# Seven block products for fourteen of sixteen pairs in the second product of an MLP

## The chip, the cores and the metric

The kernel runs on one core of one Trainium2 chip. The metric is the device time of one execution in microseconds (us), as the median over repeated executions. A core has TensorE (matrix products, writing to PSUM), VectorE, ScalarE and GpSimd for elementwise work, and SyncE, which issues the transfers between device memory and SBUF in this kernel. In the rows of the profile they are called PE (PEld for the loading of weights), DVE, ACT, POOL and SP. Each engine works through its own instructions in order and waits on the others by semaphores.

## The reference

One layer of a diffusion backbone: a recurrent branch and a Fourier branch, merged and projected, and then an MLP. The part that matters here is the MLP on 1024 tokens of width 1024, hidden width 4096:

```
h   = modulate(rms_norm(x), shift, scale)
act = square(relu(h @ w1))          # 1024 x 4096
x   = x + gt2 * (act @ w2)          # gt2: one gate per output column
out = rms_norm(x, g_final)
```

All data is float32.

## The kernel before

*How a product is formed.* A float32 operand is split into two parts of TensorE's `fp32r` format: `hi`, a copy rounded by ScalarE, and `lo`, the remainder, subtracted by VectorE (`split`, L97 to L98). A product is three passes (hi x hi, hi x lo, lo x hi), each a matmul of 128 x 128 weights against 128 x 512 columns, added up in PSUM.

*First product of the MLP* (class `Pair`, L906 to L1005). It runs over 16 pairs of feature tiles (a feature tile is 128 hidden features), each pair by seven block products instead of eight (the products `p1` to `p7`, 12 matmuls each). Each pair's results come together on VectorE: L986, L987, L993 and L1000 add PSUM banks into f1 and f2, L1004 squares the positive part, and L1005 stores a feature tile of `act` to device memory (`act_d`). `out3` finishes f1 and `out4` f2. The loop over pairs is a hand-written order: inside `tc.manual_schedule` the instructions of TensorE, VectorE and ScalarE stand as they are written, while SyncE and GpSimd are placed by a scheduler.

*Second product* (L1076 to L1144). Everything here is placed by the scheduler. It goes over 8 chunks of CH = 4 feature tiles. For each feature tile `load_split` (L757) loads the tile of `act_d` and the rows of `w2` into a working tile (`wr`), multiplies the `w2` rows by the gate `gt2` (L761, VectorE) and splits both (L98). For each of the eight output tiles (128 tokens x 1024 columns) the chunk's matmuls (L1099, 24 per output tile) add up in a PSUM tile (`mm`), and VectorE adds that to `x2` (L1136), which already holds the residual. So `x2` is the accumulator, read and written in each chunk. In the last chunk each output tile is finished at once by `finish`: square sum (L217, ScalarE), root and reciprocal (L211, L212), scaling (L1108) and store (L1109). The last output tile is taken in two halves (L1144 to L1152), so that its store starts early.

*Space.* SBUF pages come from pools: `pg` (by `page`), `yp` (by `ypage`, 17 of 4 KB per partition) and `wp`. PSUM holds 8 banks: in the first product as 8 single banks (`bk`), in the second as 4 tiles of two banks (`mm`, the pool "psum2"). A new tile waits until the old contents of its place have been read.

Of the kernel before, what the change touches and what calls it, by code (L numbers as in the profile page):

```python
# [17 lines left out]
F32 = mybir.dt.float32  # L18
# [6 lines left out]
P = 128  # L25
# [25 lines left out]
def block_kernel(es: ExitStack, tc: tile.TileContext, a, out):  # L51
# [27 lines left out]
    def page(shape, dt=F32, pool=None, tag="s"):  # L79
        return (pool or pg).tile(shape, dt, tag=tag, name=nm("pg"))  # L80
# [70 lines left out]
    def passes(w, x):  # L151
        return ((w[0], x[0]), (w[0], x[1]), (w[1], x[0]))
# [594 lines left out]
    with tc.tile_pool(name="yp", bufs=17, reuse_waits="tile") as yp:  # L747
        def ypage(shape, dt=F32):
            return page(shape, dt, yp, "y")
# [156 lines left out]
        class Pair:  # L906
# [96 lines left out]
            def put_out(self, t, j):  # L1003
                V.scalar_tensor_tensor(t, t, 0.0, t, ALU.max, ALU.mult)  # L1004
                dma(act_d[2 * self.n + j], t)  # L1005

        NP = FF // P // 2
        pr = [Pair(n) for n in range(NP)]
        with tc.high_priority(offset=PRIO):
# [68 lines left out]


        for i in range(KT):  # L1080
            x2[i] = page([P, D])
            dma(x2[i], x2_d[i])

        def load_act(f):
            hi, lo = ypage([P, T], F32R), ypage([P, T], F32R)
            load_split(act_d[f], hi, lo)
            return hi, lo

        def load_w2(f):
            hi, lo = page([P, D], F32R), page([P, D], F32R)  # L1090
            load_split(a["w2"][f * P:(f + 1) * P], hi, lo, gt2)
            return hi, lo

        def ff2(ps, i, f0, f1, hs=(0, 1)):
            for f in range(f0, f1):
                l2 = [t[:, i * P:(i + 1) * P] for t in av[f]]
                for j, (l, r) in enumerate(passes(l2, wv[f])):
                    for h in hs:
                        PE.matmul(ps[h], l, r[:, h * HB:(h + 1) * HB],  # L1099
                                  start=f == 0 and j == 0, stop=f == CH - 1 and j == 2)  # L1100

        def halves(ps):
            return ps[:, 0:HB], ps[:, HB:2 * HB]

        def finish(i):
            square_sum(x2[i], ssf[:, i:i + 1])
            r = rstd(ssf[:, i:i + 1])
            V.scalar_tensor_tensor(x2[i], x2[i], r, gfin, ALU.mult, ALU.mult)  # L1108
            dma(out[i * P:(i + 1) * P], x2[i])  # L1109

        CH = 4
        NC = FF // P // CH
        ssf = tiny(8)
        for c in range(NC):
            av, wv = [], []
            for f in range(CH):
                with tc.high_priority(offset=PRIO):
                    av.append(load_act(c * CH + f))
                    wv.append(load_w2(c * CH + f))
            pss = [mm_ps() for _ in range(2)]  # L1120
            for f0, f1 in ((0, CH - 1), (CH - 1, CH)):
                for i in range(2):
                    ff2(halves(pss[i]), i, f0, f1)
            if c == NC - 1:
                gfin = wr_tile()
                dma(gfin, a["g_final"].partition_broadcast(P))
            for i in range(KT):
                if c == NC - 1 and i == KT - 1:
                    psl = [mm_ps()[:, 0:HB] for _ in range(2)]
                    for h in range(2):  # L1130
                        ff2(psl, i, 0, CH, (h,))
                else:
                    if i >= 2:
                        pss.append(mm_ps())
                        ff2(halves(pss[i]), i, 0, CH)
                    V.tensor_tensor(x2[i], x2[i], pss[i], ALU.add)  # L1136
                if c == NC - 1 and i:
                    finish(i - 1)
        i = KT - 1
        hs = (slice(0, HB), slice(HB, D))  # L1140
        xg = wr_tile()
# [101 lines left out]
```

## Time and profile of the kernel before

| | |
|---|---|
| median of 3 runs | 1492.56 us (1491.32 to 1495.24) |
| the profiled execution | 1492.06 us |
| its span, first to last instruction | 1490.3 us |
| mean granted clock of TensorE | 0.989 |
| PE busy | 1433.6 us (96%) |
| PEld busy | 1163.7 us (78%) |
| DVE busy | 975.3 us (65%) |
| ACT busy | 552.7 us (37%) |
| POOL busy | 13.0 us (1%) |

Busy times are sums over the whole span; the second product of the MLP fills the last 365 us of it. An engine's busy share says little by itself: what matters in a stage is which engine the others wait for. [...]

### The profile page before, as it was taken

How to read it: one execution, taken by the hardware profiler on the slowest of the kernel's cores; microseconds unless marked ns; L12 is line 12 of the kernel's file. 1: busy time of each engine (PE TensorE's matmuls, PEld its weight loads, DVE VectorE, ACT ScalarE, POOL GpSimd, SP SyncE). 2: the span in 40 equal slices, each digit the busy share in tenths (PEclk: the TensorE clock that was granted, in tenths of full speed). 3: DMA queues.
4: the chain of work that ended last, by engine and by line, in shares of the span. 5: the costliest groups of instructions: out<-in, count | busy, mean ns of one | idle time of the engine just before them, and what ended most of it. 6: DMA issues, size and time to landing. Idle time of an engine off the chain costs nothing. (4 is left out here: it accounts for less than half of the span.)

```text
span 1490.3 us, 16239 instructions
## 1 busy us (share of the span) xinstructions
PE 1433.6 (96%) x6520; PEld 1163.7 (78%) x6520; DVE 975.3 (65%) x1141; ACT 552.7 (37%) x683; POOL 13.0 (1%) x14
## 2 busy tenths in 40 slices
PE   4999999999999999999995999999998999999998
PEld 3888888888888877888774778888877888888886
DVE  7664648888987898546566776666677654455524
ACT  7443245775576647221244212222223221112102
POOL 0000000000000000000002000000000000000000
PEclk9999999999999999999997999999999999999999
DMA  8433611334224334649321343322358332133202
GB/s 326 182 113 117 236 43 57 115 129 144 82 90 129 116 123 131 206 129 338 113 96 36 132 141 105 102 106 97 105 171 294 128 103 75 51 111 113 71 0 113
DMA packets 54475, 188.89 MB, mean 127 GB/s; under 512 B 6084, under 2 KB 6492, under 8 KB 54400
## 3 DMA queue, kind: packets, MB, share of 16 engines
q1 hardware_dynamic: 54399, 187.86, 36.9%
q8 instruction: 51, 0.84, 0.2%
q14 instruction: 25, 0.20, 0.0%
HBM read 150.60 MB, written 37.23 MB: 126 GB/s over the span
## 5 line engine op out<-in xcount | busy, mean ns | idle before, releaser
L1099 PE MATMUL mm<-pg,pg 128*128 128x512 f32 x1536 | 358.5, 396 | 3.9 <-DVE pg L98 3.9
L1099 PEld LDWEIGHTS mm<-pg,pg 128*128 128x128 f32 x1536 | 289.6, 189 | 72.6 <-DVE pg L98 4.3
L321 PE MATMUL mm<-pg,wh 128*128 128x512 f32 x1120 | 309.1, 397 | 0.5 <-DVE pg L98 0.5
L321 PEld LDWEIGHTS mm<-pg,wh 128*128 128x128 f32 x1120 | 204.9, 189 | 44.0 <-DVE pg L98 1.4
L958 PE MATMUL bk<-pg,wh 128*128 128x512 f32 x720 | 226.0, 395 | 2.2 <-DVE wr L297 1.1
L98 ACT ACTIVATE pg<-wr 128x1024 fp32r<-128x1024 f32 (+1 forms) x114 | 102.8, 932 | 272.0 <-PE mm L1099 166.9
L321 PE MATMUL mm<-pg,wl 128*128 128x512 f32 x560 | 175.4, 394 | 0.0
L1136 DVE TENSOR_TENSOR pg<-pg,mm 128x1024 f32<-128x1024 f32 x63 | 76.2, 1218 | 132.2 <-PE mm L1099 132.1
L958 PEld LDWEIGHTS bk<-pg,wh 128*128 128x128 f32 x720 | 134.9, 188 | 35.2 <-DVE wr L297 2.1
L958 PE MATMUL bk<-pg,wl 128*128 128x512 f32 x360 | 141.6, 393 | 0.0
L98 DVE TENSOR_TENSOR pg<-wr,pg 128x1024 fp32r<-128x1024 f32 (+1 forms) x114 | 121.2, 1087 | 29.8 <-ACT pg L98 29.4
L98 DVE TENSOR_TENSOR wl<-wr,wh 128x1024 fp32r<-128x1024 f32 (+2 forms) x73 | 81.6, 1120 | 75.8 <-ACT wh L98 75.8
L98 ACT ACTIVATE wh<-wr 128x1024 fp32r<-128x1024 f32 (+2 forms) x73 | 71.0, 975 | 147.8 <-PE mm L321 68.5
L321 PEld LDWEIGHTS mm<-pg,wl 128*128 128x128 f32 x560 | 105.4, 188 | 24.2
L859 PE MATMUL mm<-pg,pg 128*128 128x512 f32 x384 | 91.9, 397 | 0.0
L958 PE MATMUL bk<-pg,pg 128*128 128x512 f32 x264 | 73.3, 429 | 19.2 <-ACT pg L98 15.1
L859 PEld LDWEIGHTS mm<-pg,pg 128*128 128x128 f32 x384 | 71.0, 188 | 17.8 <-DVE g L893 2.2
L958 PEld LDWEIGHTS bk<-pg,pg 128*128 128x128 f32 x264 | 53.2, 206 | 36.0 <-ACT pg L98 19.0
L958 PEld LDWEIGHTS bk<-pg,wl 128*128 128x128 f32 x360 | 67.6, 188 | 16.0
L98 ACT ACTIVATE wh<-pg 128x1024 fp32r<-128x1024 f32 x32 | 33.6, 1063 | 112.1 <-PE bk L958 52.7
L776 PE MATMUL mm<-pg,wh 128*128 128x512 f32 x256 | 70.0, 394 | 1.7 <-ACT pg L98 1.7
L217 ACT ACTIVATE jk<-pg 128x1024 bf16<-128x1024 f32 (+1 forms) x27 | 27.6, 1021 | 108.3 <-DVE pg L1136 66.9
(231 smaller groups left out, 1679.9 us busy)
## 6 DMA issues: line engine op xcount, KB each, us to landing
wr<-in_w SPq DMA_DIRECT2D x67, 512.0 KB, 4.1
wr<-in_win SPq DMA_DIRECT2D x36, 512.0 KB, 4.4
pg<-in_wm SPq DMA_DIRECT2D x32, 512.0 KB, 8.3
wr<-in_wm SPq DMA_DIRECT2D x32, 512.0 KB, 3.8
act_d<-pg SPq DMA_DIRECT2D x32, 512.0 KB, 2.8
wr<-act_d SPq DMA_DIRECT2D x32, 512.0 KB, 4.2
pg<-in_x SPq DMA_DIRECT2D x16, 512.0 KB, 8.0
gyb_d<-l SPq DMA_DIRECT2D x8, 512.0 KB, 4.0
```

What stands on the lines that cost most here:

```text
L98: return S.activation(hi, src, AF.Copy), V.tensor_tensor(lo, src, f32(hi), ALU.subtract)
L217: S.activation(j[:, 0:src.shape[1]], src, AF.Square, accum_out=dst)
L321: PE.matmul(ps[:, h * HB:(h + 1) * HB], l[:, k, :], r[:, h * HB:(h + 1) * HB], start=k == 0 and i == 0, stop=k == KT - 1 and i == 2)
L776: PE.matmul(ps[:, h * HB:(h + 1) * HB], l[:, k, :], r[:, h * HB:(h + 1) * HB], start=k == 0 and i == 0, stop=k == KT - 1 and i == 2)
L859: PE.matmul(ps, l, r, start=k == 0 and j == 0, stop=k == KT - 1 and j == 2)
L958: PE.matmul(ps, l, r, start=first and k == 0 and i == 0, stop=k == 3 and i == 2, skip_group_check=not first)
L1099: PE.matmul(ps[h], l, r[:, h * HB:(h + 1) * HB], start=f == 0 and j == 0, stop=f == CH - 1 and j == 2)
L1136: V.tensor_tensor(x2[i], x2[i], pss[i], ALU.add)
```

## The change

The second product is written anew as a class `Mlp2`. Take a pair of feature tiles. Its `act` part is a 2 x 2 matrix of blocks (two halves of the tokens, two feature tiles), its `w2` part another (two feature tiles, two halves of the columns). The product of the two is formed by seven block products (Strassen's scheme in Winograd's form), for 14 of the 16 pairs. The pairs are taken in three chunks of 5, 5 and 4; the seven products of a chunk are *units* (`units`, 21 of them), and a unit is 12 matmuls per pair, added up over the pairs of the chunk in two PSUM tiles.

- *Operands.* Four loads per pair bring page tiles x, y, z, w of 1024 columns, each holding a 512-column block of `act_d` and a 512-column block of `w2` (L1042, L1043: DMAs of 256 KB with rows of 2 KB). Sums and differences of blocks are formed in place: L1068, L1070, L1072 on VectorE (1024 wide), L1074 and L1076 on GpSimd (512 wide). Each unit's operands are split (L98) into a ring of 17 tiles.
- *Accumulators.* Each of the seven products has two tiles `acc` of 1024 columns in SBUF. After a unit ScalarE copies PSUM there in the first chunk (L1094), and VectorE adds PSUM to it in the two others (L1096).
- *End.* 14 additions (L1107) turn the seven accumulators into four blocks; GpSimd multiplies them by the gate (L1113, 16 times 512 wide). The last two pairs, four feature tiles, are taken plainly as before (`plain`, `plain_mm`, gated on GpSimd, L1119). Per output tile VectorE adds two halves of accumulators (L1163) and a PSUM tile (L1167) to `x2`, and `finish` (L1014, L1015) follows.
- *Order.* `begin()` (loads, first splits and sums) is written ahead of `pr[15].out4()`, and all of `run()` lies inside the manual schedule. The gain `g_final` is loaded into `gacc`.

```diff
+        class Mlp2:
+            CHUNKS, NPL = ((0, 5), (5, 5), (10, 4)), 2
+            SRC = {"x": (0, 0, 1, 1), "y": (1, 0, 0, 1), "z": (1, 1, 0, 0), "w": (0, 1, 1, 0)}
+            RING = ("wr",) * 4 + ("y",) * 3 + ("wh", "wl") * 3 + ("s",) * 4
...
+            def load(self, c, names, new=page, ks=None):
+                n0, g = self.CHUNKS[c]
+                for k in ks or range(g):
+                    for n in names:
+                        r, ca, cb, d = self.SRC[n]
+                        t = self.src[c][n][k] = new([P, 2 * HB])
+                        f = 2 * (n0 + k)
+                        dma(t[:, 0:HB], act_d[f + ca][:, r * HB:(r + 1) * HB])
+                        dma(t[:, HB:], a["w2"][(f + cb) * P:(f + cb + 1) * P, d * HB:(d + 1) * HB])
...
+                    if u == 1:
+                        p["s"][k] = page([P, 2 * HB])
+                        V.tensor_tensor(p["s"][k], x, y, ALU.subtract)
+                    elif u == 2:
+                        V.tensor_tensor(y, y, z, ALU.add)
+                    elif u == 3:
+                        V.tensor_tensor(y, y, x, ALU.subtract)
+                    elif u == 4:
+                        G.tensor_tensor(z[:, HB:], w[:, HB:], y[:, HB:], ALU.subtract)
+                    elif u == 5:
+                        G.tensor_tensor(x[:, 0:HB], w[:, 0:HB], y[:, 0:HB], ALU.subtract)
...
+            def evac(self, i):
...
+                for j, ps in enumerate(self.ps.pop(i)):
+                    if c == 0:
+                        self.acc[u].append(ypage([P, 2 * HB]))
+                        S.activation(self.acc[u][j], ps, AF.Copy)
+                    else:
+                        V.tensor_tensor(self.acc[u][j], self.acc[u][j], ps, ALU.add)
+
+            def begin(self):
+                self.load(0, "xz", ypage, range(2))
+                self.load(0, "xz", page, range(2, 5))
+                self.split(0)
+                self.load(0, "y")
+                self.sums(1)
...
+            def gate(self, u, d):
+                for j in range(2):
+                    t = self.acc[u][j].rearrange("p (a b) -> p a b", b=HB)
+                    for h in range(2):
+                        G.tensor_tensor(t[:, h], t[:, h], gt2[:, d * HB:(d + 1) * HB], ALU.mult)
+
+            def plain(self, f):
...
+                G.tensor_tensor(rw, rw, gt2, ALU.mult)
...
+            def run(self):
...
+                for i, (c, u) in enumerate(self.units):
+                    self.evac(i - 1)
+                    if u == 1:
+                        self.load(c, "w")
+                    if u >= 4 and c + 1 < nc_:
+                        self.load(c + 1, "xyz"[u - 4])
+                    self.split(i + 1)
+                    self.sums(i + 2)
+                    if c + 1 == nc_ and u >= 3:
+                        self.plain(f0 + u - 3)
+                    self.mm(i)
...
+                self.comb(Q6, Q6, Q1, ALU.add)
+                self.comb(Q7, Q6, Q7, ALU.subtract)
+                self.comb(Q4, Q4, Q7, ALU.add)
+                self.gate(Q4, 0)
+                self.comb(Q7, Q5, Q7, ALU.subtract)
+                self.gate(Q7, 1)
+                self.comb(Q2, Q2, Q1, ALU.add)
+                self.gate(Q2, 0)
+                self.comb(Q5, Q5, Q6, ALU.subtract)
+                self.evac(nu - 1)
+                self.comb(Q3, Q3, Q5, ALU.add)
+                self.gate(Q3, 1)
+                C = ((Q2, Q3), (Q4, Q7))
+                for n, i in enumerate(order):
+                    for h in range(2):
+                        s = slice(h * HB, (h + 1) * HB)
+                        t = self.acc[C[i // 4][h]][i % 4 // 2][:, i % 2 * HB:(i % 2 + 1) * HB]
+                        V.tensor_tensor(x2[i][:, s], x2[i][:, s], t, ALU.add)
+                    if n < KT - 1:
+                        ps = mm_ps()
+                        self.plain_mm(halves(ps), i, (0, 1))
+                        V.tensor_tensor(x2[i], x2[i], ps, ALU.add)
...
+                    if n:
+                        finish(order[n - 1])
...
+            mlp2.begin()
             pr[NP - 1].out4()
-        psum_pool("psum2", 4)
...
+            psum_pool("psum2", 4)
+            mlp2.run()
```

What the change moves is seen in the order of three engines. First SyncE's transfers around the store of the last pair's first feature tile (`act_d<-pg_7932` before, `act_d<-pg_7933` now, both L1005). Before, loads of the residual (`x_d`) and of the next feature tiles stand there:

```order
L759 DMA wr_8086<-act_d 128x1024
L1082 DMA pg_8028<-x_d 128x1024
L1082 DMA pg_8030<-x_d 128x1024
L759 DMA wr_8092<-in_w 128x1024
L1005 DMA act_d<-pg_7932 128x1024
L1082 DMA pg_8032<-x_d 128x1024
L1005 DMA act_d<-pg_7965 128x1024
```

Now (pg_8081 is the y tile of the first pair, pg_8042 and pg_8048 are z tiles, pg_8045 an x tile):

```order
L1042 DMA pg_8039<-act_d 128x512
L1043 DMA pg_8039<-in_w 128x512
L1005 DMA act_d<-pg_7933 128x1024
L1042 DMA pg_8042<-act_d 128x512
L1043 DMA pg_8042<-in_w 128x512
L1042 DMA pg_8045<-act_d 128x512
L1043 DMA pg_8045<-in_w 128x512
L1042 DMA pg_8048<-act_d 128x512
L1043 DMA pg_8048<-in_w 128x512
L1042 DMA pg_8081<-act_d 128x512
L1043 DMA pg_8081<-in_w 128x512
```

The first loads of the stage stand on both sides of the store; three of the ten x and z tiles and all y tiles stand behind it.

Then VectorE at the end of the first product. Before, with bk_7938 and bk_7952 the PSUM banks of the last pair:

```order
L987 TENSOR_TENSOR pg_7965<-pg_7965,bk_7952 128x512
L98 TENSOR_TENSOR pg_8085<-wr_8086,pg_8084 128x1024
L1000 TENSOR_TENSOR pg_7932<-pg_7933,bk_7952 128x512
L1004 SCALAR_TENSOR_TENSOR pg_7932<-pg_7932 128x1024
L993 TENSOR_TENSOR pg_7965<-pg_7933,bk_7938 128x512
L1004 SCALAR_TENSOR_TENSOR pg_7965<-pg_7965 128x1024
L761 TENSOR_TENSOR wr_8092<-wr_8092,gt_5873 128x1024
L98 TENSOR_TENSOR pg_8052<-wr_8053,pg_8051 128x1024
```

Now, with bk_7939 the bank that L993 reads and pg_8081 to pg_8093 the y tiles:

```order
L1004 SCALAR_TENSOR_TENSOR pg_7933<-pg_7933 128x1024
L98 TENSOR_TENSOR wr_8052<-pg_8021,wr_8051 128x512
...
L98 TENSOR_TENSOR wh_8076<-pg_8048,wl_8075 128x512
L1068 TENSOR_TENSOR pg_8096<-pg_8021,pg_8081 128x1024
L1068 TENSOR_TENSOR pg_8098<-pg_8027,pg_8084 128x1024
L1068 TENSOR_TENSOR pg_8100<-pg_8033,pg_8087 128x1024
L1068 TENSOR_TENSOR pg_8102<-pg_8039,pg_8090 128x1024
L1068 TENSOR_TENSOR pg_8104<-pg_8045,pg_8093 128x1024
L993 TENSOR_TENSOR pg_7966<-pg_7934,bk_7939 128x512
L1004 SCALAR_TENSOR_TENSOR pg_7966<-pg_7966 128x1024
```

L993 and the second L1004 stood right behind the first L1004; now ten half splits and five sums stand between them.

Last, VectorE at the end of the second product. Before, an addition of PSUM, a reciprocal and a scaling for each output tile:

```order
L1136 TENSOR_TENSOR pg_8032<-pg_8032,mm_9978 128x1024
L212 RECIPROCAL tiny_10039<-tiny_10039 128x1
L1108 SCALAR_TENSOR_TENSOR pg_8032<-pg_8032,tiny_10039,wr_9967 128x1024
L1136 TENSOR_TENSOR pg_8034<-pg_8034,mm_10011 128x1024
L212 RECIPROCAL tiny_10072<-tiny_10072 128x1
```

Now, behind ten further L1107 (mm_9974 and mm_9975 belong to the last block product, mm_10075 and mm_10103 to plain products, x_1503 and x_1504 are output tiles):

```order
L1107 TENSOR_TENSOR pg_8397<-pg_8397,pg_8488 128x1024
L1107 TENSOR_TENSOR pg_8399<-pg_8399,pg_8490 128x1024
L1096 TENSOR_TENSOR pg_8811<-pg_8811,mm_9974 128x1024
L1096 TENSOR_TENSOR pg_8813<-pg_8813,mm_9975 128x1024
L1107 TENSOR_TENSOR pg_8811<-pg_8811,pg_8397 128x1024
L1107 TENSOR_TENSOR pg_8813<-pg_8813,pg_8399 128x1024
L1163 TENSOR_TENSOR x_1503_10032<-x_1503_10032,pg_8589 128x512
L1163 TENSOR_TENSOR x_1503_10032<-x_1503_10032,pg_8306 128x512
L1167 TENSOR_TENSOR x_1503_10032<-x_1503_10032,mm_10075 128x1024
L1163 TENSOR_TENSOR x_1504_10034<-x_1504_10034,pg_8589 128x512
```

The additions of the last block product's PSUM tiles stand behind twelve L1107, and each output tile has two more additions.

## Rows read from the trace of the kernel before

**Rows 1.** The costliest groups of the page: busy us, mean ns | idle before, releaser.
```profile
L1099 PE MATMUL mm<-pg,pg 128*128 128x512 f32 x1536 | 358.5, 396 | 3.9 <-DVE pg L98 3.9
```
**Rows 2.** The chain that ended last, its last 400 us: start us, us, what.
```profile
1108.67 1.13 DVE wr L761
1109.81 0.61 DVE pg L977
...
1110.55 11.35 PE bk L958 x48
...
1121.92 0.70 DVE pg L993
...
1122.65 1.23 DVE pg L1004
1123.87 1.14 DVE wr L761
1125.01 1.15 DVE pg L98
...
1126.20 357.91 PE mm L1099 x1534
...
1484.13 0.70 DVE pg L1144
```
**Rows 3.** Busy time of each engine by stretches.
```profile
core 0: us, PE busy (x) PEld busy (x) DVE busy (x) ACT busy (x) POOL busy (x), PEclk, DMA share, GB/s
650.00:655.00 5.00, 5.00 (x23) 4.03 (x23) 2.43 (x3) 2.05 (x3) 0.00 (x0) 1.00 0.81 223
790.00:795.00 5.00, 4.59 (x10) 3.20 (x11) 1.57 (x2) 0.61 (x2) 0.00 (x0) 0.50 0.38 108
795.00:800.00 5.00, 4.80 (x23) 3.57 (x22) 2.51 (x3) 2.59 (x5) 1.29 (x1) 0.93 0.00 0
1126.20:1131.80 5.60, 5.60 (x17) 4.44 (x18) 3.35 (x3) 0.00 (x0) 0.00 (x0) 0.70 0.97 364
1131.00:1136.00 5.00, 5.00 (x24) 4.02 (x23) 0.00 (x0) 0.00 (x0) 0.00 (x0) 1.00 1.03 419
1200.00:1300.00 100.00, 100.00 (x432) 80.89 (x432) 49.49 (x42) 16.09 (x16) 0.00 (x0) 1.00 0.27 85
```
**Rows 4.** Timeline of DVE at the end of the first product: start us, us.
```profile
1119.16 0.69 DVE L1000 TENSOR_TENSOR pg<-pg,bk 128x512 f32<-128x512 f32 x1
1119.88 1.23 DVE L1004 SCALAR_TENSOR_TENSOR pg<-pg 128x1024 f32<-128x1024 f32 x1
```
**Rows 5.** Transfers of the page: count, KB each, us from issue to landing.
```profile
act_d<-pg SPq DMA_DIRECT2D x32, 512.0 KB, 2.8
```
**Rows 6.** Groups by line and form from 1050 us to the end.
```profile
L98 DVE TENSOR_TENSOR pg<-wr,pg 128x1024 fp32r<-128x1024 f32 x64 | 76.2, 1221 | 26.5 <-ACT pg L98 26.3
L1136 DVE TENSOR_TENSOR pg<-pg,mm 128x1024 f32<-128x1024 f32 x63 | 76.2, 1218 | 132.2 <-PE mm L1099 132.1
L98 ACT ACTIVATE pg<-wr 128x1024 fp32r<-128x1024 f32 x64 | 64.5, 1053 | 229.5 <-PE mm L1099 166.9 <-DMA wr<-act_d 56.6 <-DVE wr L761 5.8
L761 DVE TENSOR_TENSOR wr<-wr,gt 128x1024 f32<-128x1024 f32 x32 | 39.1, 1222 | 9.6 <-DMA wr<-in_w 9.5
L1108 DVE SCALAR_TENSOR_TENSOR pg<-pg,tiny,wr 128x1024 f32<-128x1024 f32 x7 | 9.0, 1284 | 0.2
```
**Rows 7.** Timeline of PE after two pauses, their idle time in brackets.
```profile
790.18 1.22 PE L958 MATMUL bk<-pg,pg 128*128 128x512 f32 x2 [7.18 <-ACT pg L98]
...
1121.73 0.62 PE L1099 MATMUL mm<-pg,pg 128*128 128x512 f32 x2
1126.20 9.03 PE L1099 MATMUL mm<-pg,pg 128*128 128x512 f32 x31 [3.85 <-DVE pg L98]
```
**Rows 8.** Timeline of POOL, 820 to 835 us.
```profile
825.40 1.29 POOL L842 TENSOR_TENSOR wr<-pg 128x512 f32<-128x512 f32 x1 [10.12 <-issue]
827.32 1.67 POOL L845 TENSOR_TENSOR wr<-pg,wr 128x512 f32<-128x512 f32 x1 [0.63 <-DVE wr L844]
```
**Rows 9.** Timeline of DVE beside it, 820 to 830 us.
```profile
824.63 0.69 DVE L843 TENSOR_TENSOR wr<-pg,pg 128x512 f32<-128x512 f32 x1 [5.86 <-ACT pg L823]
825.43 1.81 DVE L844 TENSOR_TENSOR wr<-pg,wr 128x512 f32<-128x512 f32 x1
...
828.37 1.71 DVE L98 TENSOR_TENSOR pg<-wr,pg 128x1024 fp32r<-128x1024 f32 x1 [0.52 <-ACT pg L98]
```
**Rows 10.** The queue of SP at the end.
```profile
1486.84 0.81 SPq L1152 DMA_DIRECT2D out<-wr  x2
```

More of the change, by code (lines that the diff above doesn't have):

```diff
@@ L1005, in put_out, with halves, finish, __init__ @@
                 dma(act_d[2 * self.n + j], t)
+        def halves(ps):
+            return ps[:, 0:HB], ps[:, HB:2 * HB]
+        def finish(i):
+            square_sum(x2[i], ssf[:, i:i + 1])
+            r = rstd(ssf[:, i:i + 1])
+            V.scalar_tensor_tensor(x2[i], x2[i], r, gfin, ALU.mult, ALU.mult)
+            dma(out[i * P:(i + 1) * P], x2[i])
+        class Mlp2:
+            CHUNKS, NPL = ((0, 5), (5, 5), (10, 4)), 2
+            SRC = {"x": (0, 0, 1, 1), "y": (1, 0, 0, 1), "z": (1, 1, 0, 0), "w": (0, 1, 1, 0)}
+            RING = ("wr",) * 4 + ("y",) * 3 + ("wh", "wl") * 3 + ("s",) * 4
+            def __init__(self):
+                self.units = [(c, u) for c in range(len(self.CHUNKS)) for u in range(7)]
+                self.src = [{n: [None] * g for n in "xyzws"} for _, g in self.CHUNKS]
+                self.op, self.ps, self.acc, self.slot = {}, {}, [[] for _ in range(7)], 0
+            def ring(self):
+                tag = self.RING[self.slot % len(self.RING)]
+                self.slot += 1
+                if tag in ("y", "s"):
+                    return (ypage if tag == "y" else page)([P, 2 * HB], F32R)
+                return wp.tile([P, 2 * HB], F32R, tag=tag, name=nm(tag), bufs=4 if tag == "wr" else 3)
+            def load(self, c, names, new=page, ks=None):
[7 more added lines that the diff above has]
+                        dma(t[:, HB:], a["w2"][(f + cb) * P:(f + cb + 1) * P, d * HB:(d + 1) * HB])
+            def split(self, i):
+                if i >= len(self.units):
+                    return
+                c, u = self.units[i]
+                p, self.op[i] = self.src[c], []
+                for k in range(self.CHUNKS[c][1]):
+                    hi, lo = self.ring(), self.ring()
+                    if u == 0:
+                        split(p["x"][k][:, 0:HB], hi[:, 0:HB], lo[:, 0:HB])
+                        split(p["z"][k][:, HB:], hi[:, HB:], lo[:, HB:])
+                    else:
+                        split(p["_syyzwx"[u]][k], hi, lo)
+                    self.op[i].append((hi, lo))
+            def sums(self, i):
+                if i >= len(self.units):
+                    return
+                c, u = self.units[i]
+                p = self.src[c]
+                for k in range(self.CHUNKS[c][1]):
+                    x, y, z, w = (p[n][k] for n in "xyzw")
+                    if u == 1:
[9 more added lines that the diff above has]
+                        G.tensor_tensor(x[:, 0:HB], w[:, 0:HB], y[:, 0:HB], ALU.subtract)
+            def mm(self, i):
+                self.ps[i] = [mm_ps() for _ in range(2)]
+                op, t = self.op.pop(i), [h for ps in self.ps[i] for h in halves(ps)]
+                for k, hl in enumerate(op):
+                    for j in range(4):
+                        m = [q[:, j * P:(j + 1) * P] for q in hl]
+                        for n, (l, r) in enumerate(passes(m, [q[:, HB:] for q in hl])):
+                            PE.matmul(t[j], l, r, start=k == 0 and n == 0, stop=k == len(op) - 1 and n == 2)
+            def evac(self, i):
+                if i < 0:
+                    return
+                c, u = self.units[i]
+                for j, ps in enumerate(self.ps.pop(i)):
+                    if c == 0:
+                        self.acc[u].append(ypage([P, 2 * HB]))
+                        S.activation(self.acc[u][j], ps, AF.Copy)
+                    else:
+                        V.tensor_tensor(self.acc[u][j], self.acc[u][j], ps, ALU.add)
[5 more added lines that the diff above has]
+                self.sums(1)
+            def comb(self, d, s0, s1, op):
+                for j in range(2):
+                    V.tensor_tensor(self.acc[d][j], self.acc[s0][j], self.acc[s1][j], op)
+            def gate(self, u, d):
+                for j in range(2):
+                    t = self.acc[u][j].rearrange("p (a b) -> p a b", b=HB)
+                    for h in range(2):
+                        G.tensor_tensor(t[:, h], t[:, h], gt2[:, d * HB:(d + 1) * HB], ALU.mult)
+            def plain(self, f):
+                ra, rw = page([P, T]), page([P, D])
+                dma(ra, act_d[f])
+                dma(rw, a["w2"][f * P:(f + 1) * P])
+                G.tensor_tensor(rw, rw, gt2, ALU.mult)
+                t = [page([P, T], F32R) for _ in range(4)]
+                split(ra, t[0], t[1])
+                split(rw, t[2], t[3])
+                self.pl.append((t[:2], t[2:]))
+            def run(self):
+                nu, nc_, self.pl = len(self.units), len(self.CHUNKS), []
+                f0 = 2 * sum(self.CHUNKS[-1])
+                for i, (c, u) in enumerate(self.units):
[9 more added lines that the diff above has]
+                    self.mm(i)
+                order = (4, 5, 6, 7, 0, 1, 2, 3)
+                Q1, Q7, Q5, Q6, Q4, Q2, Q3 = range(7)
+                for j in range(KT):
+                    x2[j] = wp.tile([P, D], F32, tag=self.RING[(0, 1, 2, 3, 7, 8, 9, 10)[j]], name=nm("x2"),
+                                    bufs=4 if j < 4 else 3)
+                    dma(x2[j], x2_d[j])
+                dma(gfin, a["g_final"].partition_broadcast(P))
+                self.comb(Q6, Q6, Q1, ALU.add)
[20 more added lines that the diff above has]
+                        V.tensor_tensor(x2[i], x2[i], ps, ALU.add)
+                    else:
+                        self.last = i, [mm_ps()[:, 0:HB] for _ in range(2)]
+                        for h in range(2):
+                            self.plain_mm(self.last[1], i, (h,))
+                    if n:
+                        finish(order[n - 1])
+            def plain_mm(self, ps, i, hs):
+                for f, (av, wv) in enumerate(self.pl):
+                    for j, (l, r) in enumerate(passes([t[:, i * P:(i + 1) * P] for t in av], wv)):
+                        for h in hs:
+                            PE.matmul(ps[h], l, r[:, h * HB:(h + 1) * HB],
+                                      start=f == 0 and j == 0, stop=f == 2 * self.NPL - 1 and j == 2)
@@ L1007, in block_kernel @@
+        ssf, gfin, mlp2 = tiny(8), gacc, Mlp2()
         NP = FF // P // 2
@@ L1094, in ff2 @@
[L1094 to L1138, printed above, removed]
@@ L1139, in block_kernel @@
-        i = KT - 1
+            psum_pool("psum2", 4)
+            mlp2.run()
+        i, psl = mlp2.last
         hs = (slice(0, HB), slice(HB, D))
-        xg = wr_tile()
+        xg = ypage([P, D])
         st = tiny(2)
```

11 lines of the change are left out of this document (removed).

## The prediction

> **What bounds the kernel now.** I read the costliest groups of the page first: the 1536 matmuls of the second MLP product (L1099) hold TensorE for 358.5 us, with 3.9 us of idle time ahead of them [rows 1]. The chain of waits comes next. The reader is to see that from 1126.20 us one block of 357.91 us, all L1099, runs to the end, that ahead of it stand four VectorE operations (1121.92 to 1126.15) during which TensorE waits, and behind it a short tail [rows 2]. The stage table comes third: in the steady stretch 432 matmuls pass in 100 us, 0.2315 us each, with VectorE 49% and ScalarE 16% busy and GpSimd idle [rows 3]. So the stage is bound by TensorE. VectorE has about 50 us of slack in each 100, and a change that trades matmuls for VectorE work is paid out of that slack until it is used up.
>
> **The change, part by part.** I call E the end of the last matmul of the first product: 1121.90 in the chain. One wait ahead of it, 1109.81 to 1110.55 on L977, stands behind a gate and a split of the old stage (L761, L98) [rows 2]. In the new order of VectorE these two no longer stand ahead of L977, so I take E = 1121.2.
>
> *Matmuls.* 14 pairs x 7 products x 12 are 1176, and four plain feature tiles x 8 x 2 x 3 are 192: 1368 instead of 1536. 168 x 0.232 = 39.0 us saved. A matmul is the same 128x512 instruction as before.
>
> *Start of the stage.* SP's order decides it. The store of the last pair's first feature tile (waiting for L1004, which ends 0.8 us before E [rows 4]) stands ahead of six loads of x and z and of the ten loads of y; with the store these are 4.6 MB. VectorE's order does the rest: the five sums of L1068, which need y, stand ahead of the last pair's L993. TensorE's 7th matmul of the new stage writes a PSUM tile over the bank that L993 reads. So TensorE does 6 matmuls behind E and then waits for the fifth y, one sum and L993. In the first 10 us of the old stage the queues moved 364 to 419 GB/s at a DMA share near 1 [rows 3]: 11 to 13 us, and with 2 to 2.8 us of flight (a 512 KB store lands 2.8 behind its issue [rows 5]) the last y is there at E + 12.5 to 15. A sum takes 1.22 (as L1136 does [rows 6]) and L993 0.69 [rows 2]: I take a restart at E + 15.5. The price on the other side: these loads have rows of half the length, and in a stretch that mixes such loads with long ones 223 GB/s went with a share of 0.81, 275 at a full share [rows 3]; that gives E + 20. I take the value near the first rows, since the burst is the same kind as theirs. Idle time is then 15.5 - 1.4 = 14.1 against 3.85 before, the gap between 1126.20 and the first two matmuls of L1099 [rows 7].
>
> After 7.2 us of idle time [rows 7] the granted clock was 0.50 over 790 to 795 and 0.93 over the next 5 us, some 2.8 us lost; before, in the first 5.6 us of L1099, 0.70, so 1.7 lost [rows 3]. The start costs 10.2 + 1.1 = 11.3 us more than now.
>
> *The block products.* A unit is one of the seven products of a chunk: with five pairs 60 matmuls, 13.95 us. VectorE does in a unit at most 10 splits or sums of 1024 elements at 1.22 and two additions of PSUM at 1.22 [rows 6]: 14.6. GpSimd gets 10 subtractions of 512 per chunk at 1.29 each [rows 8], 4 plain gates, and later 16 gates. In the trace these two engines don't run beside each other: while GpSimd's L842 ran (825.40 to 826.69) VectorE's L844 took 1.81, and a 512-wide operation otherwise takes 0.69 [rows 8, 9]; a split beside L845 took 1.71 instead of 1.22. Where operations follow each other, they start 1.14 apart [rows 2]. So a GpSimd operation between SBUF tiles is counted on VectorE's time. The additions of PSUM read one SBUF operand less; I count them as free of this.
>
> [...]
>
> Added up unit by unit, the first two chunks (c0's sums go to ScalarE) leave VectorE behind by no unit's length, so no matmul waits. In the third chunk, with four pairs and 11.16 us a unit, six units give 67 us of matmuls; VectorE has 12 additions, 24 splits, 8 sums and 8 plain splits, 62.7 us, and GpSimd 8 x 1.29 + 4 x 2.5 = 20.3, of which 4.5 lie beside additions of PSUM: 78.5. VectorE starts the last unit 11.5 us late. Stalls inside the stage: 0 to 2 us, I take 1.
>
> *The tail.* Before, TensorE set the pace to the last matmul, and 6.2 us followed. Now VectorE does. From the start of the last block product (call it T): 11.5 of arrears; 12 of 14 additions L1107 between SBUF tiles, 12 x 1.14 = 13.7; beside them seven gates of GpSimd at 1.29, 9.0; two additions of PSUM, 2.4; the last two L1107 and two gates, 4.9; then eight result tiles, each with two 512-wide additions, one of PSUM and one L1014 (1.28, as L1108 [rows 6]). The first two tiles 6.6 and four of the gates left 5.2, 11.8; five more at 0.69 x 2 + 1.22 + 1.28 and a reciprocal, about 4 each, 19.9; the last with its halves and its own scaling 6.9, the store 3.25 (from 1486.84 to the span's end at 1490.3, about the same [rows 10]). Sum: 83.3, say 84. TensorE alone would need 48 + 192 matmuls, 55.7, and 6.2 behind them: 62. TensorE is held in the middle of it: four PSUM tiles exist, so its third plain tile waits for the additions of PSUM that stand behind twelve L1107. The tail costs 22 us more than TensorE's own pace.
>
> *Edits at about nothing.* The earlier load of the final gain and the loads of x2 have over 60 us of lead. ScalarE has 42 more splits and 14 copies, at 1.05 each [rows 6] some 60 us over 270, beside matmuls: its busy share stays below 50%, and if it were late a unit's split would move by one operation, 1 us. The 32 gates of w2 (39.1 us, L761) leave VectorE; they lay beside matmuls and give nothing by themselves.
>
> *Sum.* E 1121.2, restart 1136.7; then 1176 - 6 - 48 = 1122 matmuls at 0.232, 260.3, plus 2.8 of clock and 1 of stalls: T = 1400.8. T + 84 = 1484.8 for the span, against 1490.3: 5.5 less. The same from the terms: -39.0 - 0.7 + 11.3 + 1 + 22 = -5.4. The profiled execution took 1492.06, 1.8 outside its span and 0.5 below the median of 1492.56. So I forecast **1487 us** (1492.06 - 5.5 = 1486.6).
>
> **The rivals.**
> *GpSimd beside VectorE costs little.* If the two met only at the start of an operation, the 20.3 us of the third chunk's GpSimd work and the gates of the tail would fall out of VectorE's path: arrears of 11.5 gone, 9.0 less in the gates, and TensorE's 62 as the floor: about 17 us less, 1470. Against it stand both meetings of rows 8 and 9, which agree to 0.1 us. Chance 0.15.
> *The start is no longer than now.* If y came in time, 10.6 us fall away: 1476.5. That needs loads issued before E, and SP's order has them behind the store. Chance 0.07.
> *Slower: GpSimd also holds the additions of PSUM, and an operation costs it more than 1.29.* L845 took 1.67 where it met VectorE [rows 8]. With 1.65 each, 24 operations of 512 from the third chunk on cost 8.6 more, the plain gates 2.9, and the 4.5 of overlap and the additions between the gates, some 6 in all, go: 17 to 18 more, 1504. It decides from about 1.45 per operation with the overlap gone (24 x 0.16 + 4 x 0.32 = 5.1, and a part of the 6): the gain of 5.5 is then used up. For it speaks that all of VectorE's slack is planned away; against it that 1.67 contains the wait for a split. Chance 0.20.
> *That it doesn't do what it says:* the order holds 1368 matmuls, so this has no chance worth a number.
> The forecast keeps 0.58, between 1480 and 1494 by its own bounds: the start E + 13.5 to E + 20 (-2, +4.5), arrears and stalls 4 either way.
>
> **How the numbers follow.** 0.3%, about 4.5 us, is what a measurement of this kernel can tell from no change, so *faster* is below 1488 and *slower* above 1497. Faster: 0.15 + 0.07 and 0.32 of the forecast's 0.58, 0.54. Same: 0.22 of the forecast and 0.03 of the slower rival, 0.25. Slower: 0.04 and 0.17, 0.21. The range 1471 to 1503 leaves out half of the first rival and half of the slower one.
>
> **What would show it right or wrong.** In the profile after: 1368 matmuls in two groups; one gap of 13 to 15 us on TensorE ahead of the 7th matmul, released by L993, with L1068 waiting for loads of y; clock near 0.5 for about 5 us; matmuls without gaps over 260 us; GpSimd's 512-wide operations at 1.29 to 1.7 and VectorE's neighbours of them at about 1.8; VectorE idle less than a few us from the third chunk to the end; idle time on TensorE at the third plain tile, released by L1096 or L1167. Wrong if the gap at the start is below 6 or over 20 us, if matmuls wait inside chunks, or if VectorE finishes the last block product's additions before T + 30.

## The result and the profile after

The changed kernel takes **1470.57 us** (median of 4 runs, 1469.69 to 1471.51), the kernel before 1492.05 beside it: a ratio of 0.9852 (95% interval 0.9835 to 0.9869). The forecast was 1487, with a range from 1471 to 1503. The sign was right, and the gain four times the forecast's 5.5 us: the profiled execution took 1469.69 with a span of 1467.9, 22.4 less than 1490.3.

First the start of the stage, in the chain that ended last (start us, us, what). It answers to [rows 2]:

```profile
1094.99 24.76 PE bk L958 x107
...
1122.20 6.27 DMA pg<-in_w
...
1128.49 5.42 DMA pg<-in_w
...
1134.03 1.23 DVE pg L1068
...
1135.31 1.23 DVE pg L1068
...
1136.54 0.61 DVE pg L993
```

and in TensorE's timeline, which answers to [rows 7]:

```profile
1119.57 0.40 PE L1085 MATMUL mm<-wr 128*128 128x512 f32 x1
1120.29 0.72 PE L1085 MATMUL mm<-wr,wr 128*128 128x512 f32 x2 [0.32 <-DVE wr L98]
...
1137.19 0.79 PE L1085 MATMUL mm<-wr 128*128 128x512 f32 x1 [15.48 <-DVE pg L993]
```

The reader is to see the loads of y, the last two sums, L993, and TensorE waiting 15.48 us for it behind 6 matmuls: the forecast's gap, with its restart at 1137.19 against 1136.7.

Then the stages (columns as in [rows 3]):

```profile
1137.20:1142.80 5.60, 5.60 (x15) 4.39 (x16) 5.60 (x5) 1.06 (x1) 0.00 (x0) 0.56 0.61 167
1200.00:1300.00 100.00, 100.00 (x437) 81.78 (x436) 74.24 (x65) 45.07 (x49) 22.69 (x10) 1.00 0.32 107
1331.10:1397.10 66.00, 66.00 (x290) 53.97 (x289) 65.84 (x49) 27.43 (x27) 27.89 (x12) 1.00 0.25 89
1402.10:1415.80 13.70, 13.70 (x61) 11.11 (x60) 13.70 (x14) 0.00 (x0) 7.84 (x1) 1.00 0.36 136
1415.80:1442.50 26.70, 26.70 (x117) 21.66 (x116) 25.12 (x19) 4.34 (x9) 26.68 (x16) 1.00 0.06 25
```

TensorE has no gap in any of them; 437 matmuls pass in 100 us where 432 did [rows 3]. In the third chunk (third line) VectorE is busy all the time, 49 operations in 66 us. Behind the restart the granted clock, a share of full speed, was 0.56 over 5.6 us (first line): 5.6 x 0.44, 2.5 us lost.

The tail shows what was not foreseen. VectorE's timeline:

```profile
1402.12 13.71 DVE L1107 TENSOR_TENSOR pg<-pg,pg 128x1024 f32<-128x1024 f32 x12
1415.75 2.35 DVE L1096 TENSOR_TENSOR pg<-pg,mm 128x1024 f32<-128x1024 f32 x2
1418.02 3.56 DVE L1107 TENSOR_TENSOR pg<-pg,pg 128x1024 f32<-128x1024 f32 x2
1421.49 1.79 DVE L1163 TENSOR_TENSOR x<-x,pg 128x512 f32<-128x512 f32 x1
1424.48 1.77 DVE L1163 TENSOR_TENSOR x<-x,pg 128x512 f32<-128x512 f32 x1 [1.20 <-POOL pg L1113]
```

GpSimd's timeline beside it, the first gate, and below it the start of its first run in the first chunk:

```profile
1407.96 9.03 POOL L1113 TENSOR_TENSOR pg<-pg,gt 128x512 f32<-128x512 f32 x1 [8.11 <-DVE pg L1107]
```

```profile
1161.29 5.47 POOL L1074 TENSOR_TENSOR pg<-pg,pg 128x512 f32<-128x512 f32 x1 [333.89 <-DVE pg L1072]
1166.72 1.30 POOL L1076 TENSOR_TENSOR pg<-pg,pg 128x512 f32<-128x512 f32 x1
1167.97 2.35 POOL L1074 TENSOR_TENSOR pg<-pg,pg 128x512 f32<-128x512 f32 x1
1170.28 2.28 POOL L1076 TENSOR_TENSOR pg<-pg,pg 128x512 f32<-128x512 f32 x1
```

Twelve L1107 took 13.71 us, 1.14 each, although a gate had been waiting since 1407.96. That gate lasted 9.03 us: it ended with the first addition of PSUM, behind the twelve. Only then do the engines take turns: L1163 at 1.79 instead of 0.68, which it takes behind the last gate. The same is to be seen in the first chunk: 5.47 for the first L1074, until the last of five L1072 in a row was done, and 2.3 each once VectorE works again.

TensorE was never held in the tail: the 192 plain matmuls run from 1408.11 without a wait for 44.7 us, to 1452.8. VectorE goes on for 11.5 us behind that, and the end comes with it.

### The profile page after: what moved, and what is told of

Same layout as the page of the kernel before. It is cut to its first block, busy times and chain, and to the rows that moved or that the text cites. A ratio compares the mean times of both kernels' runs of the same rounds, so it can differ in the third digit from the quotient of the medians.

```text
span 1467.9 us, 16270 instructions
## 1 busy us (share of the span) xinstructions
PE 1390.6 (95%) x6352; PEld 1131.4 (77%) x6352; DVE 1058.0 (72%) x1209; ACT 611.2 (42%) x753; POOL 123.6 (8%) x62
## 5 line engine op out<-in xcount | busy, mean ns | idle before, releaser
L98 DVE TENSOR_TENSOR wl<-wr,wh 128x1024 fp32r<-128x1024 f32 (+2 forms) x73 | 81.6, 1121 | 75.5 <-ACT wh L98 75.5
L98 ACT ACTIVATE wh<-wr 128x1024 fp32r<-128x1024 f32 (+2 forms) x73 | 71.0, 976 | 147.6 <-PE mm L321 67.0
L98 ACT ACTIVATE pg<-pg 128x1024 fp32r<-128x1024 f32 (+4 forms) x86 | 75.7, 901 | 64.5 <-PE mm L1085 13.3
L98 ACT ACTIVATE wh<-pg 128x1024 fp32r<-128x1024 f32 x48 | 50.2, 1061 | 125.7 <-PE bk L958 52.6
L98 DVE TENSOR_TENSOR pg<-pg,pg 128x1024 fp32r<-128x1024 f32 (+4 forms) x71 | 81.0, 1157 | 20.0 <-ACT pg L98 19.9
L859 PE MATMUL mm<-pg,pg 128*128 128x512 f32 x384 | 91.9, 397 | 0.0
L859 PEld LDWEIGHTS mm<-pg,pg 128*128 128x128 f32 x384 | 71.0, 188 | 17.9 <-DVE g L893 2.2
L98 DVE TENSOR_TENSOR wl<-pg,wh 128x1024 fp32r<-128x1024 f32 x48 | 58.0, 1223 | 28.0 <-ACT wh L98 28.0
L1074 POOL TENSOR_TENSOR pg<-pg,pg 128x512 f32<-128x512 f32 x14 | 37.5, 2676 | 476.8 <-DVE pg L1072 476.8
L842 POOL TENSOR_TENSOR wr<-pg 128x512 f32<-128x512 f32 x4 | 5.7, 1424 | 810.5 <-ACT pg L823 800.5
L1085 PE MATMUL mm<-pg,pg 128*128 128x512 f32 x224 | 69.7, 392 | 0.0
```

The source lines that it names most:

```text
L98: return S.activation(hi, src, AF.Copy), V.tensor_tensor(lo, src, f32(hi), ALU.subtract)
L842: G.tensor_tensor(t34[:, 0], b22, b12, ALU.subtract)
L859: PE.matmul(ps, l, r, start=k == 0 and j == 0, stop=k == KT - 1 and j == 2)
L1074: G.tensor_tensor(z[:, HB:], w[:, HB:], y[:, HB:], ALU.subtract)
L1085: PE.matmul(t[j], l, r, start=k == 0 and n == 0, stop=k == len(op) - 1 and n == 2)
```

## The experiments

The times below are medians beside runs of the kernel before (1493.34 for e1 to e3, 1492.93 for e5 and e6, 1492.10 for e7), so ratios are to be compared, with 0.9852 for the changed kernel; gains in us are taken from them. The three small kernels (m1 to m3) were executed once each. The question was whether the forecast's rule (each GpSimd operation costs VectorE its 1.29 us) or another one rules the two engines, and how much of the time the start and the gates hold.

**Turns, measured by themselves (m1_turns).**

```
for i in range(12):
    V.tensor_tensor(A[i], A[i], B, ALU.add)      # or another kind
    if i == 1: gates()                           # 6 GpSimd products of 128x512
```

> A kernel of its own, without the layer: blocks of 12 VectorE operations of 128x1024, beside 6 GpSimd products of 128x512 that start behind the second of them. Adds between SBUF tiles alone; GpSimd alone; the same adds beside GpSimd; subtractions with a rounded result, without a wait on another engine; adds that wait for ScalarE copies made long before; adds of a PSUM tile; adds with a one-element operation between them. The forecast's rule (each GpSimd operation costs VectorE 1.29 us): the 12 take 13.7 + 6 x 1.29 = 21.4 us in every block but the ones alone and with PSUM. Theory of turns (a run of VectorE operations that waits for no other engine keeps GpSimd out; one that waits for another engine lets it in): the plain run takes 13.7 us and the first contending GpSimd operation lasts over 8 us, the rounded run the same, and the run that waits for ScalarE alternates: about 2.3 us for each VectorE and each GpSimd operation while both go on, some 20 us in all. If it is the rounded result that lets GpSimd in, the rounded run alternates and the waiting one doesn't. PSUM: 13.7 us and GpSimd at 1.29 each, or, if additions of PSUM contend too, as one of the others.

VectorE's blocks (start us, us):

```profile
19.18 13.68 DVE L56 TENSOR_TENSOR acc<-acc,bop 128x1024 f32<-128x1024 f32 x12
...
40.55 20.10 DVE L64 TENSOR_TENSOR acc<-acc,bop 128x1024 f32<-128x1024 f32 x12
...
60.71 20.09 DVE L71 TENSOR_TENSOR rem<-acc,bop 128x1024 fp32r<-128x1024 f32 x12
...
80.80 13.70 DVE L77 TENSOR_TENSOR acc<-acc,cop 128x1024 f32<-128x1024 f32 x12
...
101.82 13.65 DVE L83 TENSOR_TENSOR acc<-acc,mm 128x1024 f32<-128x1024 f32 x12
```

GpSimd's beside the plain adds, the waiting adds and the adds of PSUM:

```profile
43.05 2.11 POOL L47 TENSOR_TENSOR gat<-acc,gt 128x512 f32<-128x512 f32 x1 [2.61 <-DVE acc L64]
45.12 11.04 POOL L49 TENSOR_TENSOR gat<-gat,gt 128x512 f32<-128x512 f32 x5
...
83.28 12.33 POOL L47 TENSOR_TENSOR gat<-acc,gt 128x512 f32<-128x512 f32 x1 [9.24 <-DVE acc L77]
...
104.31 1.27 POOL L47 TENSOR_TENSOR gat<-acc,gt 128x512 f32<-128x512 f32 x1 [2.60 <-DVE acc L83]
```

Three things follow. In turns six gates cost VectorE 20.10 - 13.68 = 6.4 us, 1.07 each, not 1.29. Twelve additions of PSUM lose nothing beside six gates, 13.65 against 13.68 for the plain adds alone, and GpSimd beside them nothing either: 1.27 for the first gate, 1.26 alone. And a run can keep GpSimd out (12.33 for the first gate, VectorE at 13.70) - but in the block where my theory of turns expected turns, and not in the plain one where it expected none. That theory fell.

In the block with 12.33 GpSimd waited not for one operation of VectorE but for ten, to the end of the run at 94.50.

**The start (e1_out4_second).**

```diff
-            mlp2.begin()
-            pr[NP - 1].out4()
+            mlp2.begin(pr[NP - 1].out4)
...
                     self.op[i].append((hi, lo))
+                    if between and k == 0:
+                        between()
```

> The changed kernel with out4 of the last pair written behind the first pair's half splits, ahead of the other splits and the five sums. Theory (the start waits for L993 behind the loads of y, 15.5 us idle and 2.5 of clock): the gap falls to 0 to 3 us, the block products start at once, y is there before the second unit needs it, and the time falls by 13 to 17 us, to about 1455. Rival (y is late for the second unit too, the wait only moves): a gap of over 8 us before the second unit and a gain under 7 us.

Measured 1459.07, ratio 0.9769 (0.9755 to 0.9784), 12 us faster than the changed kernel. The gap of 15.48 is gone; TensorE's timeline has in its place, ahead of the second unit:

```profile
1139.84 0.50 PE L1087 MATMUL mm<-wh,wl 128*128 128x512 f32 x1 [3.90 <-DVE wh L98]
```

That split stands behind five sums, the last of which waits for the last load of y. The stage behind it (columns as in [rows 3]):

```profile
1139.80:1145.40 5.60, 5.56 (x17) 4.43 (x18) 5.60 (x6) 1.82 (x2) 0.00 (x0) 0.70 0.63 229
```

The gain is less than the 13 to 17 us expected, and the rows say why: the wait of 3.90 stayed, and behind it the granted clock was 0.70 over 5.6 us, 1.7 us lost. 15.48 + 2.5 less 3.90 + 1.7 is 12.4, the measured gain. So the start cost what the forecast said, and the theory holds but for this wait, which also lies below the rival's 8 us.

**No gates (e2_no_gates).** The products L1113 are left out, so the block products enter ungated.

```diff
-                        G.tensor_tensor(t[:, h], t[:, h], gt2[:, d * HB:(d + 1) * HB], ALU.mult)
+                        pass
```

> The changed kernel without the 16 products of GpSimd with the gate at the end (L1113); the block products then enter ungated. Theory (the tail is VectorE's, and the gates lengthen its operations by about 10 us between 1418 and 1445, and not the twelve combining additions): those twelve take 13.7 us as now, the result tiles come about 10 us earlier, but TensorE's last matmul (1452.8) and 6.2 us behind it are the floor: 8 to 9 us less, about 1462. Rival (VectorE's own work sets the tail, gates cost nothing): within 2 us of 1470.

Measured 1462.49, 0.9793 (0.9779 to 0.9808): 8.8 us less than the changed kernel, as the theory says. VectorE's timeline:

```profile
1402.21 13.71 DVE L1107 TENSOR_TENSOR pg<-pg,pg 128x1024 f32<-128x1024 f32 x12
1415.83 2.35 DVE L1096 TENSOR_TENSOR pg<-pg,mm 128x1024 f32<-128x1024 f32 x2
1418.09 2.36 DVE L1107 TENSOR_TENSOR pg<-pg,pg 128x1024 f32<-128x1024 f32 x2
1420.36 1.29 DVE L1163 TENSOR_TENSOR x<-x,pg 128x512 f32<-128x512 f32 x2
```

The twelve L1107 take the same 13.71 without a gate. The gates cost nothing there. Behind them the fifth tile's first addition comes at 1434.67, where it came at 1446.26 with gates: 11.6 us for 16 gates, 0.7 each and not 1.29. The kernel gains less than these 11.6 because TensorE's last plain matmuls now set the end, as the theory had it.

**Gates on VectorE (e3_gates_dve).** `V.tensor_tensor` for `G.tensor_tensor` in the same line.

> The changed kernel with the 16 products with the gate at the end on VectorE instead of GpSimd, at about 0.62 us each, 10 us. The forecast's rule (a gate on GpSimd costs VectorE 1.29, 20.6 in all): 10 us less on VectorE, down to the floor of TensorE, 8 to 9 us faster, about 1462. Theory of turns (the gates on GpSimd cost VectorE about 10 us in the tail): the two cancel, 1469 to 1473, and TensorE waits 0 to 3 us ahead of its third plain tile.

Measured 1471.01, 0.9853 (0.9836 to 0.9869): no change, as the theory says, where the forecast's rule gave 8 to 9 us. But the time comes out by another path. TensorE's timeline, and a piece of the chain that ended last:

```profile
1424.13 6.06 PE L1179 MATMUL mm<-pg,pg 128*128 128x512 f32 x16 [4.83 <-DVE pg L1096]
```

```profile
1424.13 30.20 PE mm L1179 x120
```

TensorE waits 4.83 us ahead of its third plain tile for L1096, more than the 0 to 3 expected: this is the wait that the forecast had put into the changed kernel, and here it comes with the gates in VectorE's own queue. The end hangs on this wait and the matmuls behind it, no longer on VectorE's sum. So the equal time refutes the forecast's rule, but does not by itself confirm the theory's 10 us.

**What lets GpSimd in (m2_waits).** Blocks of 8 operations beside 5 gates, with the waits varied.

> A kernel of its own as the one before it: blocks of 8 VectorE operations of 128x1024 beside 5 GpSimd products of 128x512. It tells apart what lets GpSimd in: (1) adds with a second operand of their own and no wait, (2) adds that wait only for VectorE's own earlier results, (3) subtractions into another tile that wait only for ScalarE's copies, long done, (4) adds that wait for both, (5) adds in place that wait only for ScalarE. If a wait on VectorE's own earlier results keeps GpSimd out, blocks 2 and 4 take 9.1 us with a first GpSimd operation of over 6 us, and 1, 3 and 5 alternate, about 14.5 us. If any wait keeps it out, only block 1 alternates. If it is the second operand (each add its own tile), 1 and 5 keep it out, 2 doesn't. The forecast's rule gives 9.1 + 5 x 1.29 = 15.6 in all five.

All five blocks took turns, 14.5 us each; none of the explanations holds. The one first gate that was kept out stood in the lead-in, 24 plain adds:

```profile
42.34 7.85 POOL L43 TENSOR_TENSOR gat<-acc,gt 128x512 f32<-128x512 f32 x1 [41.90 <-DVE acc L53]
...
57.68 2.11 POOL L43 TENSOR_TENSOR gat<-acc,gt 128x512 f32<-128x512 f32 x1 [2.61 <-DVE acc L59]
```

The idle times in brackets differ, and sorting all first operations by them gave the next question.

**Idle time (m3_idle).**

```
for lead in (10, 1, 6, 2, 8, 3, 7, 4, 5, 14, 1, 9):
    lead adds; then 3 gates beside 9 more adds
```

> A kernel of its own as the two before it: twelve blocks, in each of them VectorE adds of 128x1024 between SBUF tiles without a break, and 3 GpSimd products of 128x512 that start behind 1 to 14 of these adds, so that GpSimd has been idle for about 3 to 17 us; 9 more adds follow. So far a first GpSimd operation was kept out to the end of the run where GpSimd had been idle for 8.1 us or more, and was let in at once (2.1 to 2.2 us) where it had been idle for 6.3 us or less. If the idle time decides, the blocks with 1 to 4 leading adds take turns (first operation about 2.1 us, VectorE loses 1.1 us for each of the three), those with 7 and more keep it out (first operation 8 to 10 us, VectorE loses nothing), in whatever order they stand. If something else decides, the two kinds don't sort by idle time.

GpSimd's timeline, the first gate of four of the twelve blocks, in the order in which they ran:

```profile
26.54 8.92 POOL L45 TENSOR_TENSOR gat<-acc,gt 128x512 f32<-128x512 f32 x1 [11.69 <-DVE acc L43]
...
41.50 2.11 POOL L45 TENSOR_TENSOR gat<-acc,gt 128x512 f32<-128x512 f32 x1 [2.62 <-DVE acc L43]
...
158.09 2.11 POOL L45 TENSOR_TENSOR gat<-acc,gt 128x512 f32<-128x512 f32 x1 [6.03 <-DVE acc L43]
...
177.45 8.92 POOL L45 TENSOR_TENSOR gat<-acc,gt 128x512 f32<-128x512 f32 x1 [12.84 <-DVE acc L43]
```

The twelve sort by idle time without exception: idle for 2.62 to 6.03 us, 2.11 each (five blocks); idle for 11.69 to 17.39, 8.92 each (seven). 8.92 is where VectorE itself had to wait for the gate, since its eighth add behind it writes the tile that the gate reads. But in these blocks VectorE's run grows with GpSimd's idle time, so they do not tell which of the two decides. A meeting that stands in the kernel before, and in the changed one (there 1.81, out of a pause of 781.09 us), speaks against the idle time. GpSimd's timeline of the kernel before and VectorE's beside it:

```profile
783.19 1.82 POOL L842 TENSOR_TENSOR wr<-pg 128x512 f32<-128x512 f32 x1 [781.89 <-DMA wr<-in_w]
```

```profile
781.53 2.36 DVE L98 TENSOR_TENSOR wl<-pg,wh 128x1024 fp32r<-128x1024 f32 x2 [0.48 <-ACT wh L98]
783.81 1.75 DVE L843 TENSOR_TENSOR wr<-pg,pg 128x512 f32<-128x512 f32 x1
```

GpSimd had been idle for 781.89 us and came 1.66 us after VectorE had begun a run of two splits. It was let in behind the second of them, at 1.82, and VectorE's next operation took 1.75 instead of 0.69. So a long pause of GpSimd alone does not keep it out. What sorts the meetings of the 128x512 operations in the kernel before, the changed one and the three small kernels, this one too, is for how long VectorE had been at operations with two SBUF operands, since its own last pause (0.1 us counts as one) or GpSimd's last operation: 4.84 us or less, and GpSimd came in behind one operation; 5.98 or more, and it was kept out. The two nearest lengths lie in m3_idle, behind the pauses of 0.1 us between two blocks; the blocks' first rows in VectorE's timeline, for the gates at 158.09 and 177.45:

```profile
153.25 0.16 DVE L41 TENSOR_TENSOR tiny<-acc,gat 128x1 f32<-128x1 f32 x1
...
171.47 0.16 DVE L41 TENSOR_TENSOR tiny<-acc,gat 128x1 f32<-128x1 f32 x1
```

No run varies this length by itself, so that it is the cause is not shown, and why it should be is open.

**Sums and splits in turn (e5_start).** On top of `out4`:

```diff
-                self.sums(1)
+                for k in range(5):
+                    self.sums(1, (k,))
+                    self.split(1, ks=(k,))
```

> out4 behind the first pair's half splits, and the sums and splits of the second unit taken in turn, pair by pair, instead of five sums and then five splits. Theory (what is left of the start is a wait of 3.9 us before the second unit for its first split, behind the fifth sum and the last load of y): that wait falls to under 1 us, another 4 to 5 us less, about 1454 to 1455. Rival (VectorE, and not the start, sets the end from the third chunk on): within 1.5 us of 1459.

Measured 1462.81, 0.9798 (0.9785 to 0.9811): slower than 1459.07 (the two intervals just part), and neither case. VectorE's timeline shows my edit's fault:

```profile
1138.82 1.22 DVE L1072 TENSOR_TENSOR pg<-pg,pg 128x1024 f32<-128x1024 f32 x1
1141.23 1.23 DVE L98 TENSOR_TENSOR pg<-pg,wl 128x1024 fp32r<-128x1024 f32 x1 [1.19 <-ACT wl L98]
1142.37 1.22 DVE L1072 TENSOR_TENSOR pg<-pg,pg 128x1024 f32<-128x1024 f32 x1
1144.78 1.23 DVE L98 TENSOR_TENSOR pg<-pg,pg 128x1024 fp32r<-128x1024 f32 x1 [1.19 <-ACT pg L98]
```

Each split now waits 1.19 us for ScalarE's copy of the sum just made: 3.55 us per pair, more than the 2.8 that TensorE takes for one. One wait of 3.90 was exchanged for five: four of 0.5 us inside the second unit, and one of 3.79 ahead of the third, 5.8 in all.

**PSUM first (e6_psum_first).** The last edit kept; in the tail L1167 stands ahead of the two L1163 of its tile, and the first two stand right behind the last L1096.

> As the run before it, and in the tail the additions of PSUM stand ahead of the additions of the gated halves, the first two of them right behind the last block product's. Theory (the gates cost VectorE time only beside operations with two SBUF operands, and nothing beside additions of PSUM): two more gates run free, 2 to 4 us less than the run before it. Rival (the toll of the gates is the same wherever they run): within 1 us of it.

Measured 1461.97, 0.9794 (0.9780 to 0.9807), 0.8 less than the run before it, which the two intervals don't tell from nothing. In the profiles the stretch from the first combining addition to the end is 64.3 against 65.8 us. The time is the rival's case, within 1 us; the 1.5 us of the two profiles lie between the rival and the theory's 2 to 4: not settled.

**All together (e7_best).** As the last, but each sum one pair ahead of its split.

```diff
+                self.sums(1, (0,))
                 for k in range(5):
-                    self.sums(1, (k,))
+                    if k < 4:
+                        self.sums(1, (k + 1,))
                     self.split(1, ks=(k,))
```

> out4 behind the first pair's half splits, the sums of the second unit one pair ahead of its splits, and in the tail the additions of PSUM first. Theory (in e5_start every split waited for ScalarE's copy of a sum that had just been made, 1.2 us for each pair; with one sum in between nothing waits): the wait before the second unit falls to under 1 us, and the time to 1452 to 1455. Rival (the wait moves to the next unit's splits): about 1459.

Measured **1453.19**, 0.9739 (0.9725 to 0.9752), 1.1% below the changed kernel and 2.6% below the one before. The time is within the 1452 to 1455 expected, and the wait before the second unit is 0.16. What is left of the waits in TensorE's timeline:

```profile
1124.12 0.73 PE L1089 MATMUL mm<-wr,wr 128*128 128x512 f32 x2 [0.32 <-DVE wr L98]
1138.66 0.50 PE L1089 MATMUL mm<-wh,wl 128*128 128x512 f32 x1 [0.16 <-DVE wh L98]
1153.56 0.50 PE L1089 MATMUL mm<-pg,wr 128*128 128x512 f32 x1 [0.81 <-DVE pg L98]
```

## Why the prediction was wrong

By its own terms, in us of the profiled execution:

| step | forecast | measured |
|---|---|---|
| end of the first product, E | 1121.2 | 1119.6 |
| restart behind L993 | 1136.7 | 1137.2 |
| clock lost behind the restart | 2.8 | 2.5 |
| 1122 matmuls to the last block product (T) | 260.3 | 257.4 |
| stalls among them | 1 | 0 |
| T | 1400.8 | 1397.1 |
| from T to the twelve L1107 | 11.5 | 5.0 |
| the twelve, with gates | 22.7 | 13.7 |
| L1096 and the last two L1107 | 7.3 | 5.7 |
| eight tiles | 38.6 | 42.9 |
| store | 3.25 | 3.5 |
| rounded up (83.35 to 84) | 0.65 | |
| end | 1484.8 | 1467.9 |

*The matmuls and the start were right.* Of the start this is shown, not argued: with `out4` moved the gap goes. E came earlier than expected, but the restart did not, since it hangs on the loads of y.

*The step that failed is "a GpSimd operation between SBUF tiles is counted on VectorE's time".* The forecast drew it from two meetings [rows 8, 9], in which GpSimd had come first or had been idle for 0.63 us; both are right, and neither was the case that decides the tail. It has two faults, and the runs show both. Beside a VectorE run that had gone on for 8.1 us without a break, GpSimd waits and VectorE pays nothing: the 9.0 us charged to the twelve additions were 0, with and without the gates (e2_no_gates). In turns the price is 1.07, not 1.29 (m1_turns). The forecast counted the additions of PSUM as free, 4.5 us of overlap in the third chunk; no row of the kernel before shows that, but m1_turns does: 13.65 us for twelve beside six gates, 13.68 for twelve plain adds alone. In the third chunk, where the forecast charged 15.8 us, the operations beside GpSimd take 10.6 us more than at 1.14 apart, summed over VectorE's rows. A part comes back: the gates that were kept out run beside the eight tiles, which take 4.3 us longer than forecast.

*VectorE's own work was counted too high as well.* 62.7 us for 52 operations is 1.2 each; they follow each other at 1.14, and 49 of them, with the 10.6 lost to GpSimd, filled 65.8 us of the 66 of the third chunk. VectorE was at its limit there, but not behind: at T it was 0.5 us from the end of the split before, and the rest of the 5.0 us to the twelve L1107 went to what stands behind T in its order, two L1096 and two splits of the last plain tile.

*TensorE's hold at its third plain tile did not come*, for the same reason: L1096 of the last block product ran 18.7 us behind T, before the second plain tile was done. The forecast had named its own sign: it would be wrong if VectorE finished these additions before T + 30; they ended at T + 21. e3_gates_dve, with the gates in VectorE's queue, has that hold, 4.83 us.

*The matmuls were faster than in the rows before*: 437 against 432 in 100 us, 2.9 us to T. Why stays open; the plain matmuls of the tail took 0.233 each (44.71 for 192).

The first rival, that GpSimd costs VectorE little, gave 1470, and was given 0.15. Its time is the measured one, its mechanism only in part: the tolls were 10.6 in the chunk and 11.6 behind the twelve additions, where it had none. By its own terms (11.5 and 9.0 off the 84) it would also have given 20.5 us less and not 17, about 1466; so that the times agree is in part luck. The slower rival is refuted in its core: additions of PSUM lost nothing to GpSimd (13.65 against 13.68, m1_turns).

## What to carry to other kernels

Two meetings of two engines are not a rule: ask of each later meeting which of the two is already running, and for how long without a break, before a price from one row is multiplied by twenty. When a stage is pulled ahead of the last steps of the one before it, write those steps ahead of the first operation that waits for a load of the new stage; here that alone is worth 12 us. Give an interleaving of two engines' steps one step in hand: in e5_start the splits of the second unit waited 1.19 us each for ScalarE's copy of the sum just made, in e7_best, with one sum in between, they did not wait.

## What the runs showed of the hardware

- VectorE operations with two SBUF operands and GpSimd operations between SBUF tiles took turns in m1_turns: twelve of the first took 20.10 us beside six of the second, 13.68 alone, so 1.07 more per turn; the six took 13.2 instead of 7.4. In turns a 128x1024 and a 128x512 took about 2.2 us each.
- A GpSimd operation that came when VectorE had been at such operations for 5.98 us or more without a pause or a turn of GpSimd waited, not for one operation, but until they stopped or an addition of PSUM came: 5.47, 9.03, 12.33, 7.85 and seven times 8.92 in the runs above. One that came after 4.84 us or less was let in behind one operation, at 1.64 to 2.35, even out of a pause of 781.89 us. Between the two lengths nothing was measured, and the cause is open.
- Even a VectorE operation on a single element per partition, between two SBUF tiles, took part in the turns: in m1_turns it took 1.22 us instead of 0.15 while GpSimd was working.
